# The four units of stream operands of an MLP, taken apart into a first and a second part

## The chip, the cores and the metric

The kernel runs on one core of one Trainium2 chip. The metric is the device time of one execution in microseconds, and the median of several executions is compared. In the rows PE is TensorE's matmul stream, PEld its weight loads, DVE is VectorE, ACT is ScalarE, POOL is GpSimd and SP is SyncE, which issues the DMAs.

## The reference, cut to what matters

The input is one sequence of 1024 tokens with 1024 features in float32. There are two layers. Layer 0 mixes the tokens by gated linear attention, layer 1 by sliding-window attention, and each mixer is followed by the same kind of MLP:

```python
def sq_relu_mlp(h, w_up, w_down):
    u = jax.nn.relu(h @ w_up)
    return (u * u) @ w_down

def reference(...):
    for layer in range(DEPTH):
        ...
        h = h + mixer(rmsnorm(h, ln_mix[layer]), ...)
        h = h + sq_relu_mlp(rmsnorm(h, ln_mlp[layer]), w_up[layer], w_down[layer])
    return rmsnorm(h, ln_final)
```

`w_up` is 1024 x 4096 and `w_down` 4096 x 1024. The change lies where the mixer's output projection ends and the product `h @ w_up` begins, so it acts once in each layer.

## The kernel before, in words

**Products.** Every float32 operand is split into a high part, rounded to fp32r by a copy on ACT, and a low part, the difference, made on DVE or POOL. One product step is three 128x128x512 matmuls (`mm3`, lines 127 to 130). The MLP multiplies 2x2 blocks with seven products in place of eight (the Winograd form). For `h @ w_up`, the blocks of the weights (a11, a12, s1 to s4, a22) are made pair by pair from columns of `w_up`; a pair is 256 of the 4096 columns, so there are 16. The blocks of the normed stream (b11, b21, b22, t1, t2, t3, t4) are made once for each layer, in the class `Blocks` (lines 545 to 625). Each of them has 512 features in two tiles, j = 0 and j = 1, of 256 features and 512 columns of tokens. A product of a pair has four steps k: k = 0 and 1 read tile j = 0, k = 2 and 3 read j = 1.

**Units.** b11 and b21 come from the first four token tiles. The other five blocks need the last four as well, and are made in four units (i, j): i = 0 takes token tiles 4 and 5, i = 1 takes 6 and 7, and j picks the features. One unit (`second_half`, lines 581 to 625) transposes 4 + 4 blocks of 128x128 into two PSUM banks, p1 and p2. From p1 it makes b12 (ACT, line 605), subtracts r11 in place (DVE, 606), copies t1 out (ACT, 607), rounds it (ACT, 608) and takes its low part (POOL, 609). Line 608 is the last that reads p1. From p2 it makes b22 (ACT, 611), then in place, one after the other, t3 (DVE 612, ACT 613, DVE 614), t2 (615, ACT 616, DVE 617) and t4 (621, 622, ACT 623, DVE 624); line 612 also reads b12, and line 624 is the last that reads p2.

**Banks.** PSUM has eight banks, handed out under four tags with two buffers each: mm, sc, tp and x2. A new tile under a tag waits until the last reader of the tile two before it is done. Units (0, 1) and (1, 1) take both of their banks from tp, units (0, 0) and (1, 0) one from tp and one from x2.

**Order of the work around the change.** The end of `mix_out` (lines 640 to 660) writes it out:

- at token tile 6: unit (0, 0);
- after the last token tile: `up_begin(0)`, unit (0, 1), `up_first(1)`, unit (1, 0), `up_second(1)`, `up_begin(2)`, `up_begin(3)`, unit (1, 1), `up_begun()`.

`up_first` is the product a11 x b11 of a pair (rows of the form ux<-hb_b11) and a copy on ACT, `up_second` is a12 x b21 (uz<-hb_b21) and a copy on ACT into the tile c, and `up_begin` is both. They need b11 and b21 alone, so four of the pairs are begun before the units are done. `up_begun` adds the four c tiles to their sums (DVE, line 753). Then `run` finishes the pairs in order. For a begun pair, `up` (lines 764 to 795) takes a bank from tp for y and multiplies s1 x t1 into it (uy<-hb_t1), then s2 x t2 (ux<-hb_t2), half of s4 x b22, s3 x t3, the other half of s4 x b22, and a22 x t4.

A planner orders each engine's instructions ahead of the run, by readiness under its own estimates and by the place in the program, and each engine then runs its list in order. `keep_in_program_order` pins the first transposition of each bank and the first step of each product behind the TensorE instruction that the program has just before it, so that on PE the order above holds. `issue_after(normed)` keeps the units' DVE instructions behind the last token tile's norm (line 178). Temporary tiles of the units (b12 with t1 in one, b22 in another), the split weights and the c tiles share 12 SBUF slots, `wt`; a slot goes out in the order of the program and its next user waits for the last one to be done.

Of the kernel before, what the change touches and what calls it, by code (L numbers as in the profile page):

```python
# [9 lines left out]
F32 = mybir.dt.float32  # L10
# [6 lines left out]
P = 128  # L17
# [34 lines left out]
def kernel(  # L52
# [5 lines left out]
    nc = tc.nc  # L58
# [27 lines left out]
    wt = Slots(wts, "wt", 12)  # L86
# [13 lines left out]
    def bank(tag, name, shape=None):  # L100
        return psum.tile(shape or [P, HALF], F32, tag=tag, name=name)
# [443 lines left out]
    class Blocks:  # L545
# [3 lines left out]
        NAMES = ("b11", "b21", "b22", "t1", "t2", "t3", "t4")  # L549

        def __init__(self, name):
            self.name, self.tiles = name, {}

        def alloc(self, op, j):
            self.tiles[op, j] = [act_block([P, 2, HALF], f"{self.name}_{op}{w}{j}", F32R) for w in ("h", "l")]
# [22 lines left out]
                        nc.scalar.copy(self.raw[j][:, :, s], src)  # L578
                    nc.vector.tensor_sub(lo[:, :, s], src, hi[:, :, s].bitcast(F32))

        def second_half(self, units, hs, alloc=raw_block, tags=("tp", "x2")):


            v = nc.vector
            work, tmps = [], []
            for i, j in units:
                if i == 0:
                    for op in ("t1", "t2", "t3", "b22", "t4"):
                        self.alloc(op, j)
                c = slice(i * 256, (i + 1) * 256)  # L590
                pq = []
                for q in range(2):
                    ps = bank(tags[q], f"{self.name}b{i}{j}_tp{q}", [P, 2, 2, P])
                    for a in range(2):
                        k = 4 * q + 2 * j + a
                        for t in range(2):
                            transpose(ps[:, a, t, :], hs[4 + 2 * i + t][:, k * P:(k + 1) * P], ident,
                                      pin=a == 0 and t == 0)
                    pq.append(ps.rearrange("p a t c -> p a (t c)"))
                tmp = [alloc([P, 2, 2, 256], f"{self.name}t{z}{i}{j}") for z in "ab"]  # L600
                tmps += tmp
                hi, lo = ({op: self.tiles[op, j][w][:, :, c] for op in self.NAMES} for w in range(2))
                work.append((*pq, hi, lo, self.raw[j][:, :, c], tmp[0][:, 0], tmp[0][:, 1], tmp[1][:, 0]))
            for p1, p2, hi, lo, r11, b12, t1, b22 in work:
                nc.scalar.copy(b12, p1)
                v.tensor_sub(p1, p1, r11)
                nc.scalar.copy(t1, p1)
                nc.scalar.copy(hi["t1"], p1)  # L608
                nc.gpsimd.tensor_sub(lo["t1"], t1, hi["t1"].bitcast(F32))
            for p1, p2, hi, lo, r11, b12, t1, b22 in work:  # L610
                nc.scalar.copy(b22, p2)
                v.tensor_sub(p2, p2, b12)
                nc.scalar.copy(hi["t3"], p2)
                v.tensor_sub(lo["t3"], p2, hi["t3"].bitcast(F32))
                v.tensor_add(p2, p2, r11)
                nc.scalar.copy(hi["t2"], p2)
                v.tensor_sub(lo["t2"], p2, hi["t2"].bitcast(F32))
                nc.scalar.copy(hi["b22"], b22)
                nc.gpsimd.tensor_sub(lo["b22"], b22, hi["b22"].bitcast(F32))
            for p1, p2, hi, lo, r11, b12, t1, b22 in work:  # L620
                v.tensor_sub(p2, hi["b21"].bitcast(F32), p2)
                v.tensor_add(p2, p2, lo["b21"].bitcast(F32))
                nc.scalar.copy(hi["t4"], p2)
                v.tensor_sub(lo["t4"], p2, hi["t4"].bitcast(F32))
            wt.back(*tmps)

    def mix_out(first, lhs_of, wo, res_of, gain, name, mlp, begun=()):
        nxt = first
        hs = {}
        for t in range(NT):  # L630
            if t < len(begun):
                ht = begun[t]
            else:
                ht = act_block([P, D], f"{name}h{t}")
                nc.sync.dma_start(ht, res_of(t))
            lhs = nxt
            if t + 1 < NT:
                nxt = lhs_of(t + 1)
            if t == 6:
                mlp.blocks.second_half([(0, 0)], hs)  # L640
            proj_tile(lhs, wo, ht, f"{name}{t}", (range(K_BEGUN, KD),) if t < len(begun) else K_ALL)
            nc.sync.dma_start(mlp.h_in[t * P:(t + 1) * P, :], ht)
            hs[t] = scaled(ht, gain, f"{name}n{t}")
            if 0 < t <= NT // 2:
                mlp.blocks.first_half(t - 1, hs.pop(t - 1))
        for z in wo:
            wt.back(*z)
        normed = last["scaled"].ins
        tmp = lambda shape, nm: wt.tile(shape, F32, nm)
        mlp.up_begin(0, "mm")  # L650
        with tc.issue_after(normed):
            mlp.blocks.second_half([(0, 1)], hs, tmp, ("tp", "tp"))
        mlp.up_first(1, "mm")
        with tc.issue_after(normed):
            mlp.blocks.second_half([(1, 0)], hs, tmp)
            mlp.up_second(1, "sc")
            mlp.up_begin(2, "sc")
            mlp.up_begin(3, "x2")
            mlp.blocks.second_half([(1, 1)], hs, tmp, ("tp", "tp"))
            mlp.up_begun()  # L660

    wo += proj_weights(a_w_out[0], "wo", 3, KD, (KD - 1,))
# [341 lines left out]
    mlp = Mlp(0)  # L1004
# [129 lines left out]
    units = {}  # L1134
# [227 lines left out]
```

## Time and profile before

| | us |
|---|---|
| median of 3 runs | 2079.53 |
| lowest and highest | 2077.93, 2080.47 |
| the profiled execution | 2081.03 |
| its span in the profile | 2078.9 |
| TensorE busy in the span | 1998.2 |
| VectorE busy | 1534.1 |
| ScalarE busy | 975.9 |
| GpSimd busy | 257.2 |

The profile is of one execution. Times in the rows count from the start of its span, which leaves out 2.1 us of the 2081.03 us around it. A row of a timeline has the start, the duration, the engine, the line of the kernel, the operation and its tiles, `xN` where N like instructions that follow each other are merged, and in square brackets how long the engine had been idle before and whose end it was waiting for. In the MLP of layer 0 the tiles of the units are called hb0b_tp, hb0ta and hb0tb, in layer 1 hb1b_tp, hb1ta and hb1tb. A line of `second_half` has four rows in each layer, in the order of the units (0, 0), (0, 1), (1, 0), (1, 1).

### The profile page before, as it was taken

Reading aid. Unit: us, or ns where it says so; the run is one execution under the profiler, and the core shown is the slowest. Engines: PE = TensorE matmul, PEld = TensorE weight load, DVE = VectorE, ACT = ScalarE, POOL = GpSimd, SP = SyncE. Lnnn points to the kernel's source line nnn. Section 1 sums busy time; section 2 is a strip of 40 time slices with the busy share of each in tenths; the row PEclk is TensorE's granted clock in tenths of the full one; section 3 lists DMA queues with packets and bytes.
Section 4 is the critical chain, followed back from the end, with each engine's and each line's share of the span. In section 5 each row is a group of like instructions: output and inputs, shape, how many; then the busy total and the mean of one; then the engine's idle time right before and its main releaser. Section 6 shows DMA issues by size and latency. Waiting matters only on the chain.

```text
span 2078.9 us, 27179 instructions
## 1 busy us (share of the span) xinstructions
PE 1998.2 (96%) x9498; PEld 1659.1 (80%) x9498; DVE 1534.1 (74%) x2915; ACT 975.9 (47%) x2116; POOL 257.2 (12%) x318
## 2 busy tenths in 40 slices
PE   5899999998999999999999999999999999999997
PEld 5778888787788888888887788877778888888885
DVE  4877776748877767887785677756887776877787
ACT  5534432426555444233336677844554454423343
POOL 2222322102000000000010344622000000000000
PEclk9999999999999999999999999999999999999999
DMA  4216210422555668945512011322365667965412
GB/s 138 71 32 92 61 41 31 122 92 71 203 194 175 203 235 341 386 177 184 179 41 102 26 32 42 107 81 92 111 228 188 203 206 279 412 236 209 171 57 81
DMA packets 176808, 308.25 MB, mean 148 GB/s; under 512 B 14176, under 2 KB 110592, under 8 KB 176672
## 3 DMA queue, kind: packets, MB, share of 16 engines
q1 hardware_dynamic: 176672, 306.52, 43.5%
q8 instruction: 75, 1.23, 0.2%
q14 instruction: 61, 0.50, 0.1%
HBM read 202.67 MB, written 103.81 MB: 147 GB/s over the span
## 4 chain that ended last, share of the span: by engine, by line
PE 84%; DVE 8%; DMA 3%; ACT 2%; issue 2%; POOL 0%; SPq 0%; DVEq 0%; ACTq 0%; POOLq 0%
PE ux L106 15%; PE dx L106 14%; PE vg L106 8%; PE uy L106 7%; PE dy L106 7%; PE qT L106 4%; PE op L106 4%; PE dz L106 4%; PE uz L106 4%; PE bo L106 3%; PE ex L106 2%; PE scqk L106 2%; PE sc L106 1%; PE mmqk L106 1%; PE pt L111 1%
## 5 line engine op out<-in xcount | busy, mean ns | idle before, releaser
L106 PE MATMUL dx<-dt,ds 128*128 128x512 f32 x672 | 154.9, 389 | 0.6 <-ACT dt L691 0.6
L106 PEld LDWEIGHTS dx<-dt,ds 128*128 128x128 f32 x672 | 125.9, 188 | 27.6 <-ACT dt L691 1.4
L897 DVE TENSOR_TENSOR hr<-hr,dx 128x512 f32<-128x512 f32 x160 | 108.0, 682 | 37.4 <-PE dx L106 36.6
L691 ACT CAST ds<-du 128x512 fp32r<-128x512 f32 x128 | 79.2, 619 | 115.0 <-PE dy L106 48.4
L692 DVE TENSOR_TENSOR s<-s,s 128x512 fp32r<-128x512 f32 x128 | 88.2, 693 | 47.7 <-ACT s L691 47.7
L691 ACT CAST s<-s 128x512 fp32r<-128x512 f32 x128 | 79.7, 624 | 87.5 <-PE ux L106 47.6
L691 ACT CAST db<-dw 128x512 fp32r<-128x512 f32 x96 | 55.7, 619 | 119.8 <-PE dx L106 46.6
L106 PE MATMUL vg<-wvg_hi,hna_hi 128*128 128x512 f32 x256 | 103.3, 404 | 5.3 <-DVE e L318 4.8
L106 PE MATMUL vg<-wvg_hi,hna_lo 128*128 128x512 f32 x256 | 102.0, 399 | 0.0
L106 PE MATMUL vg<-wvg_lo,hna_hi 128*128 128x512 f32 x256 | 101.9, 398 | 0.0
L106 PE MATMUL uy<-hb_t1h,s 128*128 128x512 f32 x256 | 87.1, 402 | 8.9 <-ACT hb_t1h L608 8.9
L106 PE MATMUL dz<-db,da 128*128 128x512 f32 x384 | 93.5, 389 | 0.0
L692 DVE TENSOR_TENSOR ds<-du,ds 128x512 fp32r<-128x512 f32 x128 | 87.5, 685 | 7.6 <-ACT ds L691 7.3
L106 PE MATMUL ux<-hb_t4h,a 128*128 128x512 f32 x256 | 84.6, 391 | 2.2 <-DVE u L783 2.1
L691 ACT CAST a<-wu 128x512 fp32r<-128x512 f32 x96 | 59.2, 621 | 57.0 <-PE uy L106 46.8
L106 PE MATMUL uz<-hb_b21h,a 128*128 128x512 f32 x256 | 85.6, 396 | 0.0
L106 PE MATMUL uy<-hb_b22h,s 128*128 128x512 f32 x256 | 85.3, 389 | 0.0
L106 PE MATMUL ux<-hb_t3h,s 128*128 128x512 f32 x256 | 84.1, 389 | 1.0 <-ACT u L777 1.0
L106 PE MATMUL ux<-hb_b11h,a 128*128 128x512 f32 x256 | 84.2, 390 | 0.0
L106 PEld LDWEIGHTS dz<-db,da 128*128 128x128 f32 x384 | 72.0, 188 | 15.2 <-DMA da<-uo 0.3
L106 PE MATMUL ux<-hb_t2h,s 128*128 128x512 f32 x256 | 84.1, 389 | 0.0
L691 ACT CAST dt<-dw 128x512 fp32r<-128x512 f32 x64 | 38.3, 620 | 93.2 <-PE dz L106 42.7
(390 smaller groups left out, 5654.6 us busy)
## 6 DMA issues: line engine op xcount, KB each, us to landing
uo<-uo SPq DMA_DIRECT2D x96, 512.0 KB, 4.5
da<-uo SPq DMA_DIRECT2D x96, 512.0 KB, 6.2
wu<-in_w_up_dram SPq DMA_DIRECT2D x64, 512.0 KB, 5.3
dw<-in_w_down_dram SPq DMA_DIRECT2D x64, 512.0 KB, 5.7
du<-us SPq DMA_DIRECT2D x64, 512.0 KB, 6.9
us<-us SPq DMA_DIRECT2D x32, 512.0 KB, 2.7
us<-u SPq DMA_DIRECT2D x64, 256.0 KB, 5.3
wvg_raw<-in_a_w_in_dram SPq DMA_DIRECT2D x32, 256.0 KB, 3.1
```

The lines of the kernel that those rows point to most:

```text
L106: ins = nc.tensor.matmul(*args, **kw)
L111: ins = nc.tensor.transpose(*args)
L691: nc.scalar.copy(op[:, 0], src)
L692: nc.vector.tensor_sub(op[:, 1], src, op[:, 0].bitcast(F32))
L897: nc.vector.tensor_add(h, h, ps)
```

## The change

`second_half` is replaced by two functions. `unit_first` makes a unit's p1 bank, b12 and t1. `unit_second` makes the p2 bank and all the rest. Units (0, 0) and (0, 1) call both, one behind the other, at their old places; the p2 bank of unit (0, 1) now comes from x2. The first parts of units (1, 0) and (1, 1) both stand where unit (1, 0) stood, and both take their bank from tp. The second part of (1, 0) stands between `up_begin(2)` and `up_begin(3)`, that of (1, 1) stands behind `up_begin(3)`, and both take their bank from tp. The tile with b12 is held from the first part to the second. The instructions of a unit and their number are the same.

```diff
--- before.py
+++ after.py
@@ -549,7 +549,7 @@
         NAMES = ("b11", "b21", "b22", "t1", "t2", "t3", "t4")
 
         def __init__(self, name):
-            self.name, self.tiles = name, {}
+            self.name, self.tiles, self.b12 = name, {}, {}
 
         def alloc(self, op, j):
             self.tiles[op, j] = [act_block([P, 2, HALF], f"{self.name}_{op}{w}{j}", F32R) for w in ("h", "l")]
@@ -578,51 +578,56 @@
                         nc.scalar.copy(self.raw[j][:, :, s], src)
                     nc.vector.tensor_sub(lo[:, :, s], src, hi[:, :, s].bitcast(F32))
 
-        def second_half(self, units, hs, alloc=raw_block, tags=("tp", "x2")):
-
+        def unit_bank(self, i, j, q, hs, tag):
+            ps = bank(tag, f"{self.name}b{i}{j}_tp{q}", [P, 2, 2, P])
+            for a in range(2):
+                k = 4 * q + 2 * j + a
+                for t in range(2):
+                    transpose(ps[:, a, t, :], hs[4 + 2 * i + t][:, k * P:(k + 1) * P], ident, pin=a == 0 and t == 0)
+            return ps.rearrange("p a t c -> p a (t c)")
+
+        def unit_ops(self, i, j):
+            c = slice(i * 256, (i + 1) * 256)
+            return *({op: self.tiles[op, j][w][:, :, c] for op in self.NAMES} for w in range(2)), self.raw[j][:, :, c]
+
+        def unit_first(self, i, j, hs, alloc=raw_block, tag="tp"):
+
+            if i == 0:
+                for op in ("t1", "t2", "t3", "b22", "t4"):
+                    self.alloc(op, j)
+            p1 = self.unit_bank(i, j, 0, hs, tag)
+            hi, lo, r11 = self.unit_ops(i, j)
+            tmp = self.b12[i, j] = alloc([P, 2, 2, 256], f"{self.name}ta{i}{j}")
+            b12, t1 = tmp[:, 0], tmp[:, 1]
+            nc.scalar.copy(b12, p1)
+            nc.vector.tensor_sub(p1, p1, r11)
+            nc.scalar.copy(t1, p1)
+            nc.scalar.copy(hi["t1"], p1)
+            nc.gpsimd.tensor_sub(lo["t1"], t1, hi["t1"].bitcast(F32))
+
+        def unit_second(self, i, j, hs, alloc=raw_block, tag="x2"):
 
             v = nc.vector
-            work, tmps = [], []
-            for i, j in units:
-                if i == 0:
-                    for op in ("t1", "t2", "t3", "b22", "t4"):
-                        self.alloc(op, j)
-                c = slice(i * 256, (i + 1) * 256)
-                pq = []
-                for q in range(2):
-                    ps = bank(tags[q], f"{self.name}b{i}{j}_tp{q}", [P, 2, 2, P])
-                    for a in range(2):
-                        k = 4 * q + 2 * j + a
-                        for t in range(2):
-                            transpose(ps[:, a, t, :], hs[4 + 2 * i + t][:, k * P:(k + 1) * P], ident,
-                                      pin=a == 0 and t == 0)
-                    pq.append(ps.rearrange("p a t c -> p a (t c)"))
-                tmp = [alloc([P, 2, 2, 256], f"{self.name}t{z}{i}{j}") for z in "ab"]
-                tmps += tmp
-                hi, lo = ({op: self.tiles[op, j][w][:, :, c] for op in self.NAMES} for w in range(2))
-                work.append((*pq, hi, lo, self.raw[j][:, :, c], tmp[0][:, 0], tmp[0][:, 1], tmp[1][:, 0]))
-            for p1, p2, hi, lo, r11, b12, t1, b22 in work:
-                nc.scalar.copy(b12, p1)
-                v.tensor_sub(p1, p1, r11)
-                nc.scalar.copy(t1, p1)
-                nc.scalar.copy(hi["t1"], p1)
-                nc.gpsimd.tensor_sub(lo["t1"], t1, hi["t1"].bitcast(F32))
-            for p1, p2, hi, lo, r11, b12, t1, b22 in work:
-                nc.scalar.copy(b22, p2)
-                v.tensor_sub(p2, p2, b12)
-                nc.scalar.copy(hi["t3"], p2)
-                v.tensor_sub(lo["t3"], p2, hi["t3"].bitcast(F32))
-                v.tensor_add(p2, p2, r11)
-                nc.scalar.copy(hi["t2"], p2)
-                v.tensor_sub(lo["t2"], p2, hi["t2"].bitcast(F32))
-                nc.scalar.copy(hi["b22"], b22)
-                nc.gpsimd.tensor_sub(lo["b22"], b22, hi["b22"].bitcast(F32))
-            for p1, p2, hi, lo, r11, b12, t1, b22 in work:
-                v.tensor_sub(p2, hi["b21"].bitcast(F32), p2)
-                v.tensor_add(p2, p2, lo["b21"].bitcast(F32))
-                nc.scalar.copy(hi["t4"], p2)
-                v.tensor_sub(lo["t4"], p2, hi["t4"].bitcast(F32))
-            wt.back(*tmps)
+            p2 = self.unit_bank(i, j, 1, hs, tag)
+            hi, lo, r11 = self.unit_ops(i, j)
+            first = self.b12.pop((i, j))
+            b12 = first[:, 0]
+            tmp = alloc([P, 2, 2, 256], f"{self.name}tb{i}{j}")
+            b22 = tmp[:, 0]
+            nc.scalar.copy(b22, p2)
+            v.tensor_sub(p2, p2, b12)
+            nc.scalar.copy(hi["t3"], p2)
+            v.tensor_sub(lo["t3"], p2, hi["t3"].bitcast(F32))
+            v.tensor_add(p2, p2, r11)
+            nc.scalar.copy(hi["t2"], p2)
+            v.tensor_sub(lo["t2"], p2, hi["t2"].bitcast(F32))
+            nc.scalar.copy(hi["b22"], b22)
+            nc.gpsimd.tensor_sub(lo["b22"], b22, hi["b22"].bitcast(F32))
+            v.tensor_sub(p2, hi["b21"].bitcast(F32), p2)
+            v.tensor_add(p2, p2, lo["b21"].bitcast(F32))
+            nc.scalar.copy(hi["t4"], p2)
+            v.tensor_sub(lo["t4"], p2, hi["t4"].bitcast(F32))
+            wt.back(first, tmp)
 
     def mix_out(first, lhs_of, wo, res_of, gain, name, mlp, begun=()):
         nxt = first
@@ -637,7 +642,8 @@
             if t + 1 < NT:
                 nxt = lhs_of(t + 1)
             if t == 6:
-                mlp.blocks.second_half([(0, 0)], hs)
+                mlp.blocks.unit_first(0, 0, hs)
+                mlp.blocks.unit_second(0, 0, hs)
             proj_tile(lhs, wo, ht, f"{name}{t}", (range(K_BEGUN, KD),) if t < len(begun) else K_ALL)
             nc.sync.dma_start(mlp.h_in[t * P:(t + 1) * P, :], ht)
             hs[t] = scaled(ht, gain, f"{name}n{t}")
@@ -647,16 +653,20 @@
             wt.back(*z)
         normed = last["scaled"].ins
         tmp = lambda shape, nm: wt.tile(shape, F32, nm)
+        b = mlp.blocks
         mlp.up_begin(0, "mm")
         with tc.issue_after(normed):
-            mlp.blocks.second_half([(0, 1)], hs, tmp, ("tp", "tp"))
+            b.unit_first(0, 1, hs, tmp)
+            b.unit_second(0, 1, hs, tmp)
         mlp.up_first(1, "mm")
         with tc.issue_after(normed):
-            mlp.blocks.second_half([(1, 0)], hs, tmp)
+            b.unit_first(1, 0, hs, tmp)
+            b.unit_first(1, 1, hs, tmp)
             mlp.up_second(1, "sc")
             mlp.up_begin(2, "sc")
+            b.unit_second(1, 0, hs, tmp, "tp")
             mlp.up_begin(3, "x2")
-            mlp.blocks.second_half([(1, 1)], hs, tmp, ("tp", "tp"))
+            b.unit_second(1, 1, hs, tmp, "tp")
             mlp.up_begun()
 
     wo += proj_weights(a_w_out[0], "wo", 3, KD, (KD - 1,))
```

## Rows read from the trace of the kernel before

**Rows 1.** Page, part 1: busy time of each engine, share of the span, instructions.

```profile
PE 1998.2 (96%) x9498; PEld 1659.1 (80%) x9498; DVE 1534.1 (74%) x2915; ACT 975.9 (47%) x2116; POOL 257.2 (12%) x318
```

**Rows 2.** Waits of PE, 480 to 530 us: total us, times, longest.

```profile
PE uy L106 <- ACT hb_t1h L608: 5.2, 1, 5.2
PE hb0b_tp L111 <- ACT hb_t1h L608: 1.3, 1, 1.3
```

**Rows 3.** Waits of PE, 1440 to 1490 us.

```profile
PE hb1b_tp L111 <- ACT hb_t1h L608: 3.8, 1, 3.8
PE uy L106 <- ACT hb_t1h L608: 3.7, 1, 3.7
PE ux L106 <- DVE hb_t2l L617: 0.4, 1, 0.4
```

**Rows 4.** Stretches: length, busy us (x) of PE, PEld, DVE, ACT, POOL; granted clock, DMA.

```profile
490.00:500.00 10.00, 8.67 (x43) 6.85 (x42) 8.93 (x15) 8.13 (x17) 5.63 (x4) 1.00 0.00 1
...
514.00:520.00 6.00, 6.00 (x17) 4.71 (x17) 5.67 (x10) 3.01 (x7) 1.00 (x1) 0.59 0.39 96
...
1470.00:1475.00 5.00, 4.76 (x14) 3.79 (x15) 2.49 (x4) 2.42 (x6) 1.38 (x2) 0.66 0.59 151
```

**Rows 5.** Timeline of PE, MLP of layer 0: start, us, instruction, [idle before <- releaser].

```profile
492.74 1.09 PE L111 MATMUL hb0b_tp<-ident,opn_hs 128*128 128x128 f32 x8 [1.33 <-ACT hb_t1h L608]
...
501.96 0.39 PE L106 MATMUL ux<-hb_b11h,a 128*128 128x512 f32 x1
...
507.41 1.03 PE L111 MATMUL hb0b_tp<-ident,opn_hs 128*128 128x128 f32 x8
...
513.69 0.79 PE L106 MATMUL uy<-hb_t1h,s 128*128 128x512 f32 x1 [5.25 <-ACT hb_t1h L608]
...
518.93 0.40 PE L106 MATMUL ux<-hb_t2h,s 128*128 128x512 f32 x1
```

**Rows 6.** Timeline of ACT and DVE in layer 0, lines 608, 612 and 624.

```profile
470.65 0.69 DVE L612 TENSOR_TENSOR hb0b_tp<-hb0b_tp,hb0ta 128x512 f32<-128x512 f32 x1
...
480.20 0.68 DVE L624 TENSOR_TENSOR hb_t4l<-hb0b_tp,hb_t4h 128x512 fp32r<-128x512 f32 x1
...
495.01 0.69 DVE L612 TENSOR_TENSOR hb0b_tp<-hb0b_tp,hb0ta 128x512 f32<-128x512 f32 x1
...
496.39 0.62 ACT L608 CAST hb_t1h<-hb0b_tp 128x512 fp32r<-128x512 f32 x1
...
507.64 0.68 DVE L624 TENSOR_TENSOR hb_t4l<-hb0b_tp,hb_t4h 128x512 fp32r<-128x512 f32 x1
...
513.05 0.59 ACT L608 CAST hb_t1h<-hb0b_tp 128x512 fp32r<-128x512 f32 x1
```

**Rows 7.** Timeline of PE, MLP of layer 1.

```profile
1460.08 0.39 PE L106 MATMUL ux<-hb_b11h,a 128*128 128x512 f32 x1
...
1465.53 1.03 PE L111 MATMUL hb1b_tp<-ident,bon_hs 128*128 128x128 f32 x8
...
1470.24 0.50 PE L106 MATMUL uy<-hb_t1h,s 128*128 128x512 f32 x1 [3.68 <-ACT hb_t1h L608]
...
1474.69 0.40 PE L106 MATMUL ux<-hb_t2h,s 128*128 128x512 f32 x1
```

**Rows 8.** Timeline of DVE in layer 1, lines 612 and 624.

```profile
1425.49 0.69 DVE L612 TENSOR_TENSOR hb1b_tp<-hb1b_tp,hb1ta 128x512 f32<-128x512 f32 x1
...
1434.56 0.69 DVE L624 TENSOR_TENSOR hb_t4l<-hb1b_tp,hb_t4h 128x512 fp32r<-128x512 f32 x1 [0.70 <-ACT hb_t4h L623]
...
1448.07 0.69 DVE L612 TENSOR_TENSOR hb1b_tp<-hb1b_tp,hb1ta 128x512 f32<-128x512 f32 x1
...
1452.19 0.69 DVE L612 TENSOR_TENSOR hb1b_tp<-hb1b_tp,hb1ta 128x512 f32<-128x512 f32 x1
...
1455.98 0.68 DVE L624 TENSOR_TENSOR hb_t4l<-hb1b_tp,hb_t4h 128x512 fp32r<-128x512 f32 x1
...
1464.19 0.68 DVE L624 TENSOR_TENSOR hb_t4l<-hb1b_tp,hb_t4h 128x512 fp32r<-128x512 f32 x1
```

## The prediction

> **What bounds the kernel now.** I read the page first: PE is busy 96% of the span [rows 1], so time can only be won where PE stands still or runs slowly. Next I read PE's waits around the two places of the change. Each layer has two: the transpositions of a unit wait for a line 608 (1.3 and 3.8 us), and later uy, the first product of pair 0 that needs units, waits for a line 608 too (5.2 and 3.7 us) [rows 2, 3]. Then the stretches: the granted clock is 1.00 after the 1.3 us wait, and 0.59 and 0.66 behind the waits of uy, near the lower of TensorE's two levels, 1.2 of 2.4 GHz [rows 4]. From the timeline the slow stretch can be priced. Twenty-four matmuls take 501.96 to 507.41, so twelve take 2.72 us at the full clock; the twelve of uy take 513.69 to 518.93 = 5.24 us in layer 0 and 1470.24 to 1474.69 = 4.45 us in layer 1 [rows 5, 7]. Slow clock behind uy thus costs 2.5 and 1.7 us.
>
> What does uy wait for? The row names t1 of the last unit. But the first step of uy reads tile j = 0, which units (0, 0) and (1, 0) make; the third line 608, that of (1, 0), began at 496.39 and took 0.62 us, while uy began at 513.69, behind the fourth one (513.05 + 0.59) [rows 5, 6]. What uy lacked was its bank: y comes from tp, the tile two before it there is p1 of (1, 1), and line 608 is that bank's last reader. So I read this wait as one for PSUM, not for an operand. The Trainium skill (Perfetto Trace Analysis, Identifying Performance Opportunities) says that repeated gaps on the engine that should be saturated can mean that PSUM or SBUF has run out for the next tile. By that rule an earlier t1 takes nothing off the wait, and the trace agrees, with the 16.7 us between 497.0 and 513.69.
>
> **The change, part by part.** *Banks.* The new order of tiles in tp is p1 of (0, 0), (0, 1), (1, 0), (1, 1), then p2 of (1, 0), (1, 1), then y. Counting two back: p1 of (1, 0) is free early; p1 of (1, 1) waits for line 608 of (0, 1), just as p1 of (1, 0) does now; y waits for p2 of (1, 0), so for line 624 of that unit in place of line 608 of (1, 1). The wait of uy is not removed: it gets another end.
>
> *First wait.* The same line 608 ends it, so it stays; four of the transpositions behind it (eight take 1.09 us [rows 5]) now run inside it. PE gets to the next products 0.5 us sooner and does four transpositions later on: no change in PE's sum.
>
> *When p2 of (1, 0) begins.* It stands where ux of pair 3 begins now: 501.96 in layer 0, 1460.08 in layer 1 (0.5 us earlier by the last paragraph, and 0.5 us for its own four transpositions) [rows 5, 7]. Line 611 copies it first, an ACT operation of 0.59 us like line 608 [rows 6]. So line 612 starts at about 502.6 and 1460.7.
>
> *How long 612 to 624 takes.* This is the term that decides. Seven DVE operations of 0.69 us and three ACT operations of 0.59 us follow each other [rows 6], 6.6 us if nothing comes between: the lower bound. From the start of 612 to the end of 624 the trace has 10.2 us for (0, 0) and 13.3 for (1, 0) in layer 0, and 9.8, 8.6 and 12.7 us for (0, 0), (0, 1) and (1, 0) in layer 1 [rows 6, 8]; 13.3 is the upper bound. The surplus is other DVE and ACT work that each engine's list has put between the steps. I take (0, 0)'s 10.2 and 9.8 us: that unit is worked alone, as the second part of (1, 0) now will be for its first 5.5 us, while (1, 0) now runs in among (0, 1).
>
> *So uy starts* at 502.6 + 10.2 = 512.8 against 513.69, and at 1460.7 + 9.8 = 1470.5 against 1470.24: -0.9 and +0.3 us. PE comes to it at about 507.9 and 1466.0 (four transpositions after 507.41 and 1465.53), and so waits 4.9 and 4.5 us. That is over the 3.7 us which brought the lower clock [rows 3, 4]; the slow twelve matmuls stay, at nothing.
>
> *(1, 1) afterwards.* Its second part starts four transpositions after 507.41, now about 512. t2 of (1, 1) is first read at step k = 2 of s2 x t2, six matmuls after uy's end: about 4 us after the start of uy, 517 or later. Its two DVE operations past t3 lie well inside. The wait of 0.4 us for t2 in layer 1 [rows 3] I count as gone: -0.4. If it stays, nothing is gained.
>
> *Slots.* The order of the 12 slots puts a12 of pair 3 behind b22 of (0, 1), whose last reader is POOL's line 619, and s1 and s2 of pair 0 behind the products of pair 2. PE needs that a12 only at uz of pair 3, the last twelve matmuls before 507.41, so at 504.7, and s1 at 512.8. Unit (0, 1) is worked ahead of (1, 0), whose t1 was done at 497.0, so some 7 us cover the splitting of a12, and it would cost 1.3 us (one ACT and one DVE operation of this size [rows 6]) if that cover went. s4 and s3 of pair 0 wait for the tiles of (1, 0), and are read two products after uy begins. I cost all of this at nothing; the bounds are 0 and 1.3 us.
>
> *p2 of (0, 1) in x2* finds a bank whose last user ended before token tile 6 was done: nothing, and no gain, since nobody waits for the tp bank it leaves but p1 of (1, 0), counted above. *DMAs:* the parts issue none. SP's loads of `w_up` are queued behind the last readers of pair 0's weights and can slip by the microsecond that s3 and s4 do; pair 1 needs them 12 us after uy. Nothing.
>
> *DVE.* Five of (1, 0)'s operations (612 to 621), which DVE now starts at 495.01 [rows 6] and has done before 502, move behind that point. Five times 0.69 is 3.5 us of work in the stretch that uy waits through; it is what the upper bound of 13.3 us covers.
>
> **Sum:** -0.9 + 0.3 - 0.4 = -1.0 us. Against the profiled execution's own 2081.03 us (span 2078.9 and 2.1 around it) that is 2080.0; it stood 1.5 us over the median of the runs shown, so I forecast 2078.5 for the median. A measurement of this kernel can tell about 0.2%, 4.2 us, from no change.
>
> **The rivals.** *A, the chain runs nearly bare (faster).* With five operations fewer ahead of it DVE may leave few gaps to fill. At 7.5 us, between the bound of 6.6 and the shortest row of 8.6, uy starts at 510.1 and 1468.2: -3.6 and -2.0. PE then waits only about 2.2 us each time, nearer to the 1.3 us that left the clock at 1.00 than to 3.7, so the slow matmuls go too: -2.5 and -1.7. With -0.4: 10.2 less, 2069.3. For it: (0, 1) in layer 1 took 8.6 us with another unit beside it. Against: eight units in two layers, and none near 7.5.
>
> *B, the chain is as long as (1, 0)'s is now (slower).* The steps of (1, 1)'s second part, the weights of pair 0 and the sums of pair 1 are all ready from 503 on and go into its gaps. At 13.3 and 12.7 us uy starts at 515.9 and 1473.4: +2.2 and +3.2, the t2 wait has no part, and the median is 2084.9. For it: DVE's backlog moves into just this stretch, and (1, 0) is the unit that has shown these lengths in both layers. Against: the second part has no unit ahead of it any more. It decides from a chain of about 12.5 us in both layers, where the sum passes +4.2.
>
> *C, uy waited for t1 after all (faster).* Then the change does what its order suggests: uy starts as PE comes to it, 507.9 and 1466.0, -5.8 and -4.2, and with the clock -4.2 more: 14.2 less, 2065.3. Against it stand the order of the banks and row 496.39.
>
> *D, the change does nothing, or the first wait grows.* The planner may put line 605 of (1, 0) before 607 of (0, 1) on ACT: 0.59 us on the first wait in each layer, inside the forecast's own range.
>
> **How the numbers follow.** Forecast 0.45, its own range 2075.4 to 2083.7 (chains of about 8.5 to 12.5 us). A 0.26, B 0.23, C 0.03, D 0.03. Faster takes A and C and a little of the forecast's edge, 0.30; slower B and a little, 0.24; within 0.2%: 0.46. The range reaches to A's and B's times and half a microsecond past them, 2068.5 to 2085.5; C and the far halves of A and B are left out.
>
> **What would show it.** In the profile of the changed kernel uy of pair 0 should be released by DVE's line 624, not by ACT's 608; the wait before the transpositions should still be ended by a line 608, with four transpositions ahead of it and four behind; the third lines 612 and 624 should lie about 10 us apart, starting at about 502.6 and 1460.7 of the old count; the clock should fall behind uy. A release by anything but 624 makes the bank argument wrong. A chain under 8.5 us with the clock at 1.00 is A; over 12.5 us is B. The whole prediction fails if the rest of the MLP, in other order on DVE, waits by microseconds where it doesn't now.

## The result, and the profile after

The changed kernel took 2086.54 us (median of 10 runs, 2083.65 to 2095.54), the kernel before 2075.53 us (10 runs on the same chip). The ratio is 1.0052, with a 95% interval from 1.0041 to 1.0063: slower by 10.8 us (8.5 to 13.1). The forecast of 2078.5 us and its range, which ended at 2085.5, both miss it, and so does the sign that I held likeliest.

In the changed kernel the old lines 605 to 609 are 602 to 606, 611 is 617, 612 is 618, 617 is 623 and 624 is 629; 692, 713 to 716, 753 and 783 became 702, 723 to 726, 763 and 793. The page, part 1, answers to [rows 1]:

```profile
PE 1991.5 (96%) x9498; PEld 1655.1 (79%) x9498; DVE 1538.2 (74%) x2915; ACT 975.8 (47%) x2116; POOL 258.0 (12%) x318
```

PE has no more work than before; it stands still for longer. The waits of PE, 478 to 600 us and 1440 to 1510 us, answer to [rows 2, 3]:

```profile
PE uy L106 <- DVE hb_t4l L629: 14.6, 1, 14.6
PE ux L106 <- DVE u L793: 1.3, 1, 1.3
PE hb0b_tp L111 <- ACT hb_t1h L605: 0.3, 1, 0.3
...
PE uy L106 <- DVE hb_t4l L629: 11.2, 1, 11.2
PE hb1b_tp L111 <- ACT hb_t1h L605: 3.1, 1, 3.1
```

The releaser of uy has changed from ACT's line for t1 to DVE's line 629, and its wait has grown from 5.2 and 3.7 us to 14.6 and 11.2. In the timeline of PE, layer 0 and then layer 1, which answers to [rows 5, 7], uy stands behind the last four transpositions:

```profile
484.44 1.04 PE L111 MATMUL hb0b_tp<-ident,opn_hs 128*128 128x128 f32 x8
...
503.60 0.60 PE L111 MATMUL hb0b_tp<-ident,opn_hs 128*128 128x128 f32 x4
518.83 0.77 PE L106 MATMUL uy<-hb_t1h,s 128*128 128x512 f32 x1 [14.64 <-DVE hb_t4l L629]
...
523.29 0.39 PE L106 MATMUL ux<-hb_t2h,s 128*128 128x512 f32 x1
...
1478.37 0.76 PE L106 MATMUL uy<-hb_t1h,s 128*128 128x512 f32 x1 [11.18 <-DVE hb_t4l L629]
```

Was it the operand? In the timelines of ACT and POOL the last t1 (line 605 of (1, 1), then line 606) is done 24 us before uy starts:

```profile
492.67 0.68 ACT L605 CAST hb_t1h<-hb0b_tp 128x512 fp32r<-128x512 f32 x1
...
493.43 1.30 POOL L606 TENSOR_TENSOR hb_t1l<-hb0ta,hb_t1h 128x512 fp32r<-128x512 f32 x1 [0.69 <-ACT hb_t1h L605]
```

And the timeline of DVE has unit (1, 0)'s line 618 at 500.31, its line 629 at 518.01 (layer 1: 1462.71 and 1477.55), with the work of others between:

```profile
500.31 0.69 DVE L618 TENSOR_TENSOR hb0b_tp<-hb0b_tp,hb0ta 128x512 f32<-128x512 f32 x1
500.91 1.58 DVE L723 TENSOR_TENSOR s<-wu 128x512 f32<-128x512 f32 x1
502.52 0.69 DVE L724 TENSOR_TENSOR s<-s,wu 128x512 f32<-128x512 f32 x1
503.13 0.68 DVE L702 TENSOR_TENSOR a<-wu,a 128x512 fp32r<-128x512 f32 x1
...
508.41 0.69 DVE L618 TENSOR_TENSOR hb0b_tp<-hb0b_tp,hb0ta 128x512 f32<-128x512 f32 x1
...
518.01 0.68 DVE L629 TENSOR_TENSOR hb_t4l<-hb0b_tp,hb_t4h 128x512 fp32r<-128x512 f32 x1
...
1462.71 0.69 DVE L618 TENSOR_TENSOR hb1b_tp<-hb1b_tp,hb1ta 128x512 f32<-128x512 f32 x1
...
1477.55 0.68 DVE L629 TENSOR_TENSOR hb_t4l<-hb1b_tp,hb_t4h 128x512 fp32r<-128x512 f32 x1
```

From the start of 618 to the end of 629 that is 18.4 us in layer 0 and 15.5 us in layer 1. The row at 508.41 is already the line 618 of (1, 1). Line 629 ends at 518.69 and uy starts 0.14 us behind it; in layer 1 at 1478.23, and again 0.14 us.

A stretch of DVE over the chain of layer 0 shows that the engine never rests in it (columns: length, busy us, granted clock of PE, DMA share, GB/s):

```profile
500.31:518.69 18.38, 18.35 (x29) 0.73 0.31 86
```

**Where the time went.** The two profiles start the MLP at different times, so I count from the start of unit (0, 1)'s eight transpositions in each layer (484.44 above, 487.60 in the profile of before). uy starts 34.4 us after that mark in layer 0, before 26.1; 33.7 us in layer 1, before 28.5. The first product of pair 4, behind all four begun pairs, starts 92.3 us after the mark, before 85.1, and 91.0 us, before 88.0. So the two layers have lost 7.1 + 2.9 = 10.1 us by then, and the comparison says 10.8. By the medians nothing outside this stretch is needed. At uy itself the loss is 8.3 + 5.3 = 13.6 us; 3.5 us of it come back before pair 4, 2.0 because PE is busy there for 56.54 and 56.43 us in place of 57.62 and 57.38, the rest in shorter waits.

The two profiled executions themselves took 2086.73 us (a span of 2084.6) and 2081.03 us, only 5.7 us apart: that of the changed kernel reaches the first mark 3.2 us sooner and takes 1.2 us less in the rest outside the stretch. In the profiles of this case the first mark lies anywhere from 480.3 to 487.6 us, so I take this for scatter between executions; its cause is not shown.

### The profile page after: what moved, and what is told of

Same layout as the page of the kernel before. It is cut to its first block, busy times and chain, and to the rows that moved or that the text cites. A ratio compares the mean times of both kernels' runs of the same rounds, so it can differ in the third digit from the quotient of the medians.

```text
span 2084.6 us, 27179 instructions
## 1 busy us (share of the span) xinstructions
PE 1991.5 (96%) x9498; PEld 1655.1 (79%) x9498; DVE 1538.2 (74%) x2915; ACT 975.8 (47%) x2116; POOL 258.0 (12%) x318
## 4 chain that ended last, share of the span: by engine, by line
PE 85%; DVE 8%; ACT 3%; DMA 2%; issue 2%; POOL 1%; SPq 0%; DVEq 0%; ACTq 0%; POOLq 0%
PE ux L106 15%; PE dx L106 14%; PE uy L106 8%; PE vg L106 8%; PE dy L106 7%; PE qT L106 4%; PE dz L106 4%; PE op L106 4%; PE uz L106 4%; PE bo L106 3%; PE scqk L106 2%; PE ex L106 1%; PE mmqk L106 1%; PE sc L106 1%; PE pt L111 1%
```

## The experiments

My theory: uy waits for its bank until the chain of (1, 0), lines 618 to 629, is done, and the chain is as long as the other work that stands in DVE's list between its steps. Rivals: uy waits for an operand; DVE's total work sets the end, whatever the bank; the chain is long of itself. Ratios are to the kernel before on the same chip (its medians there were 2076.5 to 2077.3 us), and can differ by up to 0.1% from the quotient of the two medians.

### The bank alone

```diff
-            b.unit_second(1, 0, hs, tmp, "tp")
+            b.unit_second(1, 0, hs, tmp, "x2")
```

> The changed kernel with one word different: p2 of unit (1, 0) lies in x2 in place of tp, so the tile two before y in tp is p1 of (1, 1), free at about 495 in layer 0. DVE's list of work is the changed kernel's own. Theory (y waits for the bank that the chain of (1, 0) holds): uy of pair 0 starts as PE comes to it, at about 504 and 1467, where it started at 518.83 and 1478.37. PE then meets the next thing that is late: t2 of (1, 0), whose line 623 begins at 510.2, and at step 2 t2 of (1, 1), 515.6, so the second product ends at about 517.7 in place of 526.0; 7 to 8 us back in layer 0 and 4 to 5 in layer 1, 11 to 13 in all, which is before by -2 to 0. Rival 1 (uy waits for an operand of its own, t1 or s1): nothing changes, +10.8 us against before. Rival 2 (DVE's backlog alone sets the end, the bank only names the wait): the waits move to t2 and t4 whole, and the time stays within 3 us of the changed kernel's, +8 to +11 against before.

Measured: 2077.23 us, ratio 1.0001 (0.9993 to 1.0010): the whole loss is gone with one bank's tag. uy has no wait; it starts 19.5 and 22.3 us after the mark. The waits of PE, 478 to 600 us:

```profile
PE ux L106 <- DVE hb_t2l L623: 6.0, 2, 3.8
...
PE ux L106 <- ACT hb_t2h L622: 1.0, 1, 1.0
```

As expected, 7.0 us of the 14.6 come back as waits for t2, which DVE's unchanged list makes late (8.0 us in layer 1). The operand falls. The backlog rival falls as it was put (+8 to +11), but it holds what remains: behind the bank stands DVE's order.

### DVE's list alone

Banks as in the changed kernel; other work is held behind (1, 0)'s last step.

```diff
-            v.tensor_sub(lo["t4"], p2, hi["t4"].bitcast(F32))
+            done = v.tensor_sub(lo["t4"], p2, hi["t4"].bitcast(F32))
             wt.back(first, tmp)
+            return done.ins
...
+            mlp.gate = b.unit_second(1, 0, hs, tmp, "tp")
             mlp.up_begin(3, "x2")
+        with tc.issue_after(mlp.gate):
             b.unit_second(1, 1, hs, tmp, "tp")
             mlp.up_begun()
...
+                with tc.issue_after(self.gate) if p in (1, 2) else ExitStack():
                     self.up(p, lambda: self.up_out(p - 1) if p else None)
```

> The changed kernel with its banks as they are; only DVE's list differs: the second part of (1, 1), the sums and splits of pairs 1 and 2 and the four additions of line 763 are held behind the last step (line 629) of (1, 0). Between 618 and 629 of (1, 0) DVE then has 3 operations of other work in place of 20. Theory (the length of the chain under the bank is other work on DVE): the chain takes 8 to 9 us in place of 18.4 and 15.5; uy is still released by line 629, but at about 508.5 in layer 0 (518.83 before this edit) with a wait of 4 to 5 us in place of 14.6, and some 5 us sooner in layer 1. t2 of (1, 1) comes 14 operations later, at about 516.5, and takes 3 us of it back: 7 to 8 us won in layer 0, 4 to 5 in layer 1, before by -2 to 0. Rival 1 (the operand): uy's start does not follow the end of the chain, or t1 comes no sooner, so the time stays at +10.8. Rival 2 (DVE's whole backlog sets the end): the operations held back are waited for in turn, the time stays within 3 us of the changed kernel's. Rival 3 (the chain is long of itself, by the hops between ACT and DVE): it stays over 13 us, and the time with it.

Measured: 2078.09 us, ratio 1.0000 (0.9991 to 1.0009). The timeline of DVE (weight lines 2 higher) from the start to the end of the chain:

```profile
497.22 0.69 DVE L618 TENSOR_TENSOR hb0b_tp<-hb0b_tp,hb0ta 128x512 f32<-128x512 f32 x1
498.57 0.69 DVE L620 TENSOR_TENSOR hb_t3l<-hb0b_tp,hb_t3h 128x512 fp32r<-128x512 f32 x1 [0.65 <-ACT hb_t3h L619]
...
504.25 0.69 DVE L629 TENSOR_TENSOR hb_t4l<-hb0b_tp,hb_t4h 128x512 fp32r<-128x512 f32 x1 [0.65 <-ACT hb_t4h L628]
```

That is 7.72 us for ten operations, and 7.72 us in layer 1 too. uy starts 0.15 us behind the end of 629, at 505.09. So the chain is not long of itself. PE's waits, 478 to 600 us:

```profile
PE uy L106 <- DVE hb_t4l L629: 3.6, 1, 3.6
PE ux L106 <- ACT u L789: 2.1, 1, 2.1
PE ux L106 <- DVE hb_t2l L623: 1.2, 1, 1.2
PE ux L106 <- DVE u L795: 0.9, 1, 0.9
```

The wait of uy is 11 us shorter. Behind it stand 4.2 us of waits for t2 and u, where the changed kernel had 1.3: the work held back is wanted later. PE also runs slower there: from uy to pair 4 of layer 0 it is busy 59.68 us at a granted clock of 0.93, in the changed kernel 56.54 us at 0.97, for as good as the same matmuls (241 and 240 records). So of the 11.6 us by which uy starts sooner 6.0 are gone at pair 4.

### A smaller dose of the same

The edit above, without the second `issue_after`: only the sums and splits of pairs 1 and 2 are held.

> As the kernel in which DVE's other work is held behind line 629 of (1, 0), but only the sums and splits of pairs 1 and 2 are held; the second part of (1, 1) and the additions of line 763 run where the planner puts them. 13 steps of DVE's list from 618 to 629 of (1, 0) in place of 10 there and 26 in the changed kernel. Theory (each operation put into the chain costs about 0.6 us): the chain takes 9 to 10.5 us, uy starts 1 to 2 us later than with all held (22.8 us after the transpositions of (0, 1) in layer 0) and 9 to 10 us sooner than in the changed kernel; t2 of (1, 1) is sooner by 3 operations and its wait goes. Before by -3 to +1. If the second part of (1, 1) and not the weights made the chain long: uy at 28 or later, before by +4 or more.

Measured: 2077.66 us, ratio 1.0008 (0.9997 to 1.0018), 0.7 us above the range that I had given, which is less than the interval. Fourteen operations from 618 to 629 (with both ends; the expectation counts the 13 steps between them):

```profile
499.34 0.69 DVE L618 TENSOR_TENSOR hb0b_tp<-hb0b_tp,hb0ta 128x512 f32<-128x512 f32 x1
...
508.05 0.68 DVE L629 TENSOR_TENSOR hb_t4l<-hb0b_tp,hb_t4h 128x512 fp32r<-128x512 f32 x1
```

The chain takes 9.39 us in both layers, uy follows at 0.14 us (25.3 us after the mark, 2.4 later than with all held). Four operations more cost 1.67 us, 0.42 each, since they also fill one of two gaps of 0.65 us in which DVE waited for ACT.

### The chain begun earlier

```diff
             mlp.up_second(1, "sc")
+            b.unit_second(1, 0, hs, tmp, "tp")
             mlp.up_begin(2, "sc")
-            b.unit_second(1, 0, hs, tmp, "tp")
             mlp.up_begin(3, "x2")
```

> The changed kernel with the second part of (1, 0) one begun pair earlier (ahead of pair 2 in place of pair 3); banks as in the changed kernel, p2 of (1, 0) in tp under y. DVE's list has 23 operations from line 618 to 629 of (1, 0), where the changed kernel has 26, and it begins some 4 us sooner. Theory (uy starts at the end of that chain, wherever it lies): uy 5 to 7 us sooner in layer 0 than in the changed kernel (28 us after the transpositions of (0, 1) in place of 34.4), 4 to 5 in layer 1, still released by line 629: 9 to 12 us less than the changed kernel, before by -2 to +2. Rival 2 (DVE's whole backlog sets the end): DVE does the same work, later waits grow, +5 to +11. Rival 1 (the operand): no change of uy.

Measured: 2078.50 us, ratio 1.0010 (1.0000 to 1.0020), at the upper end of my -2 to +2. DVE's first row here is (1, 0)'s line 618, the last one its line 629; then PE's wait:

```profile
492.31 0.70 DVE L618 TENSOR_TENSOR hb0b_tp<-hb0b_tp,hb0ta 128x512 f32<-128x512 f32 x1 [0.19 <-ACT hb0tb L617]
...
508.75 0.68 DVE L629 TENSOR_TENSOR hb_t4l<-hb0b_tp,hb_t4h 128x512 fp32r<-128x512 f32 x1
```

```profile
PE uy L106 <- DVE hb_t4l L629: 8.1, 1, 8.1
```

The chain is still 17.1 us long, with 25 operations, but it starts sooner; uy starts at its end, 29.2 and 27.9 us after the mark. uy follows the chain, wherever that lies.

### Half of the change

```diff
             b.unit_first(1, 0, hs, tmp)
+            b.unit_second(1, 0, hs, tmp, "x2")
             b.unit_first(1, 1, hs, tmp)
             mlp.up_second(1, "sc")
             mlp.up_begin(2, "sc")
-            b.unit_second(1, 0, hs, tmp, "tp")
```

> Half of the change: unit (1, 0) is worked whole where the kernel before has it (p1 in tp, p2 in x2), only the first part of (1, 1) is moved up beside it, and its second part stays behind the fourth begun pair. The tile two before y in tp is p1 of (1, 1), free early. Theory: no wait for a bank at uy, which starts at about 504 and 1467; t2 of (1, 0) is long done; PE stands at step 2 of the second product, for t2 of (1, 1), which DVE reaches at about 516 in its list: 7 to 8 us less than the changed kernel in layer 0, 4 to 5 in layer 1, so before by -3 to 0. Rival 1 (the operand): t1 is as early as in the changed kernel, no difference between the two in uy's wait, +10. Rival 2 (the backlog sets the end): +8 to +11. Rival 4 (it is the splitting of (1, 0) that costs, since its first part keeps slots and its second comes late): the time falls to before's whatever uy does.

Measured: 2079.89 us, ratio 1.0017 (1.0006 to 1.0028), slower by 3.5 us where I had expected a little gain. uy has no wait, but ux of pair 3 has one:

```profile
PE ux L106 <- DVE hb_t4l L629: 6.1, 1, 6.1
```

It is the same mechanism under the other tag. The bank of pair 3's ux is the one two back in x2, which p2 of (0, 1) holds, and that unit's line 629 now stands behind (1, 0)'s work. I had followed the ring of tp, and not that of x2.

### Half of the change, and DVE's list

The same, and the gate of the second experiment taken from (1, 1)'s line 629, with `up_begun` and the sums and splits of pairs 1 and 2 behind it.

> As the kernel with only the first part of (1, 1) moved up, and also DVE's list is reordered: sums and splits of pairs 1 and 2 and the additions of line 763 are held behind the last step of (1, 1). Theory (a bank and DVE's order, one behind the other): no wait at uy, about 504 and 1467; the second part of (1, 1) has DVE almost to itself, so t2 is done at about 508 to 509, when PE comes to it at 508.3: under 1 us of waiting. uy starts 6 us sooner than in the kernel before in layer 0 (by the count from the transpositions of (0, 1)) and 4 in layer 1, and the clock is not lowered behind it (2.5 and 1.7 us there): before by -8 to -14 us, -0.4% to -0.7%. Against it: the sums of pair 1 come later by up to 13 operations of 0.6 us, and PE wants them 12 us after uy; if they are late, 2 to 6 us come back. Rival 2 (DVE's backlog sets the end): -3 to +3. Rival 1 (the operand): no wait at uy either, since t1 is as early as before.

Measured: 2086.26 us, ratio 1.0035 (1.0023 to 1.0048), slower by 7.3 us, and far from my -8 to -14. PE's waits, 478 to 600 us:

```profile
PE ux L106 <- DVE u L795: 5.8, 4, 2.1
PE ux L106 <- DVE hb_t4l L629: 4.1, 1, 4.1
PE ux L106 <- ACT u L789: 0.9, 1, 0.9
PE ux L106 <- DVE hb_t2l L623: 0.2, 1, 0.2
```

The waits for x2 and for u together undo it. t2 is in time (0.2 us), but too much was held for too long: line 795, which empties ux of each begun pair, is late four times. Here the backlog rival is right in kind, though its own range (-3 to +3) ended below what was measured.

### Bank and list together, the least held

The first experiment's bank, and only the sums and splits of pairs 1 and 2 held, behind line 623 (t2) of (1, 1).

> As the kernel with p2 of (1, 0) in x2 (no bank wait at uy, which started 19.5 and 22.3 us after the transpositions of (0, 1), but then 7 to 8 us of waits for t2), and the sums and splits of pairs 1 and 2 are held behind the line 623 of (1, 1). t2 of (1, 1) stands 9 places sooner in DVE's list. Theory (with the bank free, the next wait is DVE's order): the t2 waits fall from 7 to 1 to 3 us in each layer; what comes back is the sums of pair 1, about 8 operations of 0.6 us later, wanted 12 us after uy. Holding all that work behind 629 of (1, 1) with another bank layout gave 4 to 5 us of later waits for line 795; here less: before by -8 to -2 us, best estimate -5. Rival 2 (DVE's backlog is the bound of this stretch from here on): what t2 gains is lost by waits behind it, before by -2 to +2.

Measured: 2071.94 us, ratio 0.9972 (0.9959 to 0.9984). Run again, on another chip:

> The same kernel as the one with p2 of (1, 0) in x2 and the work of pairs 1 and 2 held behind line 623 of (1, 1), once more on the chip of the comparison: before by -3 to -8 us if what was measured holds (ratio 0.9972).

Measured: 2068.99 us, ratio 0.9962 (0.9947 to 0.9976). It beats both kernels: by 6 to 8 us the one before, by 17 to 19 the changed one, as the ratios give it. PE's waits in the first of the two, 478 to 600 us:

```profile
PE ux L106 <- ACT hb_t2h L622: 1.8, 1, 1.8
PE ux L106 <- DVE u L794: 1.1, 2, 0.8
PE ux L106 <- ACT u L788: 1.0, 1, 1.0
PE hb0b_tp L111 <- ACT hb_t1h L605: 0.3, 1, 0.3
PE ux L106 <- DVE hb_t2l L623: 0.2, 1, 0.2
```

They sum to 4.4 us, against 16.3 us in the changed kernel and 7.9 in that before, over the same stretch.

### The order of before, with the same remedies

First the bank alone, in the kernel before:

```diff
-            mlp.blocks.second_half([(1, 1)], hs, tmp, ("tp", "tp"))
+            mlp.blocks.second_half([(1, 1)], hs, tmp, ("x2", "tp"))
```

> The kernel before with p1 of (1, 1) in x2 in place of tp; its order of work is its own. The tile two before y in tp is then p1 of (1, 0), free at 497. Theory (uy waited for its bank, and behind that wait stands a second one for t1 of (1, 1), made by lines 608 and 609 at 513 to 515): the transpositions of (1, 1) wait up to 1 us for line 624 of (1, 0); the first six matmuls of uy run at 508 to 510, the other six wait for t1 of (1, 1) until about 514 to 515, then the clock or t2 of (1, 1) at 517 to 518 ends the gain: 1 to 3 us sooner in each layer, before by -5 to -1 us. Rival 1 (only the operand counts): uy whole at 513.7, before by 0. Rival 5 (only the bank counts): uy whole at 508 to 510 with no wait in it, before by -8 to -12.

Measured: 2074.74 us, ratio 0.9995 (0.9985 to 1.0004). Of PE's waits, 478 to 600 us:

```profile
PE uy L106 <- ACT hb_t1h L608: 2.8, 1, 2.8
...
PE hb0b_tp L111 <- DVE hb_t4l L624: 0.9, 1, 0.9
PE uy L106 <- POOL hb_t1l L609: 0.8, 1, 0.8
```

So both stood there in the kernel before: the bank first, and right behind it the operand t1 of (1, 1). Then the bank and the list (pairs 1 and 2 behind line 617 of (1, 1)):

> The kernel before, in its own order of units, with both remedies: p1 of (1, 1) in x2 (y's bank is free early), and the sums and splits of pairs 1 and 2 held behind line 617 of (1, 1). It asks whether the order that the change brings is worth anything once bank and DVE's list are set right. Theory (three waits lie one behind the other: the bank, DVE's list, and then t1 of (1, 1), which only the change makes early): t1 of (1, 1) is worked from about 20 us after the transpositions of (0, 1), and its line 609 ends at about 24; the second half of uy still waits 1 to 3 us for it, t2 follows at about 28; pair 4 begins 2 to 3 us later in each layer than with the change's order and the same remedies (81.4 and 83.3 us). Before by -5 to -1, the other by 2 to 5 us better. Rival (the change's order is worth nothing; the remedies do it all): the same time as that one, before by -6. Rival (DVE is the bound): before by -1 to +2, as with the bank alone.

Measured: 2074.96 us, ratio 0.9988 (0.9977 to 0.9998): 2.5 us faster than before, where the order of the change with the same remedies is 5.8 and 7.9 us faster. uy still waits there for t1 of (1, 1), 1.1 us for line 608 and 1.1 for line 609 in each layer. So the order that the change brings is worth some 3 to 5 us, but only once the bank and DVE's list no longer hide it. The size is loose: the interval of this run overlaps that of the first measurement of the other order and lies apart from that of the second.

### One ledger for all

Worked out from the timelines as above: the start of uy and of pair 4, us after the mark, in layers 0 and 1; their sum against before; and the time against before that the ratio gives.

| kernel | uy | pair 4 | by the ledger | measured |
|---|---|---|---|---|
| before | 26.1, 28.5 | 85.1, 88.0 | | |
| changed | 34.4, 33.7 | 92.3, 91.0 | +10.1 | +10.8 |
| bank alone | 19.5, 22.3 | 86.4, 88.3 | +1.6 | +0.2 |
| list alone | 22.8, 25.1 | 86.7, 87.2 | +0.8 | 0.0 |
| smaller dose | 25.3, 27.5 | 86.8, 86.1 | -0.3 | +1.7 |
| chain earlier | 29.2, 27.9 | 87.3, 85.6 | -0.2 | +2.1 |
| half | 29.4, 28.9 | 89.8, 88.8 | +5.5 | +3.5 |
| half and list | 25.0, 27.0 | 88.8, 90.9 | +6.5 | +7.3 |
| bank and list | 19.5, 22.2 | 81.4, 83.3 | -8.5 | -5.8, -7.9 |
| before, bank | 21.7, 25.4 | 83.6, 87.1 | -2.4 | -1.0 |
| before, bank and list | 20.8, 25.3 | 84.6, 88.0 | -0.6 | -2.5 |

The two last columns agree within 2.7 us in every row; the ledger is from one execution of each kernel, and the measured figures have intervals of 2 to 3 us to either side. Read it by its columns: uy can start 6 to 7 us sooner and pair 4 still be no earlier (bank alone), since what is not waited for at uy is waited for at t2 or u, or lost in the clock (list alone).

## Why the prediction was wrong, point by point

**Right: the bank.** uy is released by line 629, 0.14 to 0.15 us behind its end, in the changed kernel and in each of the three that left p2 of (1, 0) in tp; with p2 in x2 the wait is gone. The rule of the Trainium skill that the prediction cited (Perfetto Trace Analysis, Identifying Performance Opportunities: gaps on the engine that should be saturated can mean that PSUM ran out for the next tile) is borne out by this: t1 was 24 us early and gained nothing. Rival C falls by the same rows. The bank was the first of two waits, though: with it free, the kernel before stood at t1 of (1, 1) for 3.6 us in layer 0.

**Right: the places and the small terms.** The first wait stayed, shorter (1.33 to 0.29 us, 3.77 to 3.08 us). Line 618 began 15.9 us after the mark in layer 0, against 502.6 - 487.60 = 15.0 forecast; in layer 1 18.1 against 18.9. The t2 wait went. The slots cost nothing: between 489.38 and uy PE's timeline shows no other wait. The slow matmuls behind uy stayed, 4.46 and 4.27 us for twelve, where before they took 5.24 and 4.45; a wait about three times as long made them no slower.

**Wrong: "How long 612 to 624 takes".** This was the term that decides, and I took 10.2 and 9.8 us for it, with 13.3 as the upper bound. It measured 18.4 and 15.5 us. I read the length off other units' chains, as if it belonged to the chain, and argued that the other unit's steps had made (1, 0)'s long and would be gone. What fills the gaps is whatever is ready for DVE at that time. In layer 0 it is 20 operations: 7 sums of pairs 1 and 2, 7 splits of weights, 5 steps of (1, 1)'s second part, and 1 addition of line 763. The old chain of 13.3 us had 14. In layer 1 it is 15. The chain came out 8.2 and 5.7 us longer than I took it for, and began 0.9 us late and 0.8 us early: those are the 9.2 and 5.0 us by which uy missed its forecast places.

The trace of before had rows against the choice. Unit (1, 1) was worked there with no other unit beside it or ahead of it, and its chain still took 12.45 us in layer 0:

```profile
512.45 0.68 DVE L612 TENSOR_TENSOR hb0b_tp<-hb0b_tp,hb0ta 128x512 f32<-128x512 f32 x1
...
524.22 0.68 DVE L624 TENSOR_TENSOR hb_t4l<-hb0b_tp,hb_t4h 128x512 fp32r<-128x512 f32 x1
```

In layer 1 it took 13.20 us (from 1469.00 to the end of the row at 1481.52). The sums and splits of the pairs stood between its steps, and in layer 1 a wait of 2.3 us for a load as well; the choice of 10.2 and 9.8 us used neither.

The size comes out of a count, though one made in the trace of after. The rows of the chain stand 0.60 us apart: 27 operations by 0.60 are 16.2 us, and two that took 1.58 and 1.75 us in place of 0.68 add 2.0; that is 18.2 of 18.4. In layer 1, 22 by 0.60 and 2.1 us for two slow ones are 15.3 of 15.5. So the longest old row was no bound: the bound was the work that is ready.

**Rival B was the right mechanism at too low a price.** It named most of these operations (three sums of pair 2 and the addition came on top), and still took the old 13.3 and 12.7 us as their price. I gave it 0.23 and argued against it that the second part has no unit ahead of it; the experiment that holds the weights and (1, 1) back shows that the units ahead were not what mattered. The range, which ended half a microsecond past B, was short for the same reason.

What stays open is why the planner puts (1, 0)'s steps so far apart: whether by due times or by places in the program was not tried. Nor was a list made by hand for the whole stretch.

## What to carry to other kernels

When a tile that is worked in place moves closer to the next user of its bank, price the wait as the whole chain on its engine, and count the other work that is ready there at that time, one operation after the other; the longest chain in the old trace is not a bound. Follow the ring of every tag that a moved tile enters or leaves, since a wait taken from one may come up under another. And when a bank wait is gone, look at once for what stands next in the list: here the bank and the order on VectorE gave 2.5 us by themselves, and 6 to 8 us only together with the early operand.

## What the hardware showed that I had not expected

**VectorE beside GpSimd.** Two of DVE's operations in the chain took 1.58 and 1.75 us in place of 0.68. In POOL's timeline a line 625 stands beside each, the second and the third of these rows:

```profile
494.68 1.30 POOL L625 TENSOR_TENSOR hb_b22l<-hb0tb,hb_b22h 128x512 fp32r<-128x512 f32 x1
500.65 1.30 POOL L625 TENSOR_TENSOR hb_b22l<-hb0tb,hb_b22h 128x512 fp32r<-128x512 f32 x1 [4.66 <-ACT hb_b22h L624]
506.47 1.47 POOL L625 TENSOR_TENSOR hb_b22l<-hb0tb,hb_b22h 128x512 fp32r<-128x512 f32 x1 [4.52 <-ACT hb_b22h L624]
```

The line 723 that began at 500.91 ended at 502.49, 0.54 us behind the end of the second row (501.95). The POOL operations at 493.43 (line 606, shown above) and 494.68 slowed nobody: beside the first DVE ran line 626 (493.81, 0.68 us), beside the end of the second line 629 (495.88, 0.69 us). Both read PSUM and one SBUF tile, while lines 723 and 702 read two SBUF tiles. The Trainium skill (SBUF — State Buffer, SBUF: two separate sides) says that the port pair of the two engines is held for a whole instruction, against a DVE operation with two SBUF inputs; these rows agree.

**The clock falls while PE stands.** That it would fall was forecast; that it costs no more behind 14.6 us of waiting than behind 5.2 was not. Stretches of PE in the changed kernel (length, busy us, granted clock, DMA share, GB/s):

```profile
514.00:518.80 4.80, 0.00 (x0) 0.50 0.20 48
518.80:523.30 4.50, 4.47 (x13) 0.61 0.31 91
523.30:526.00 2.70, 2.70 (x13) 1.00 0.17 49
```

It is at the lower level, 1.2 of 2.4 GHz, before uy begins (0.50), and back at the full one for the next product (1.00).
